# When the lower quarters of w_out's first pair are cast, and where one of their low halves lies

## The chip, the cores and the metric

The kernel runs on one core of one Trainium2 chip. The metric is the device time of one execution in microseconds (us). A profiled execution has a span, from its first to its last instruction, and a time of its own, a little longer than the span.

## The reference

One layer over 2048 new frames and 32 continuing ones, with 1024 features per frame, all float32:

- a normalised frame times w_in gives six streams; a gated short convolution and a pooling mixer turn them into `concat[yA, yB]`, 1024 wide
- `h = h + concat[yA, yB] @ w_out`
- `gate = sigmoid(rmsnorm(h) @ w_ple_gate)`, then `h = h + (p @ w_ple) * gate`
- a last rmsnorm gives the outputs, and the streams' states are returned as well

The change lies in the beginning of the second step, the product with w_out.

## The kernel before

**Precision.** Each float32 operand is split in two float32r parts: `hi` is a copy by ScalarE (ACT), `lo = src - hi` a subtraction by VectorE (DVE). A product is then three matmuls: hi·hi, lo·hi and hi·lo.

**The stages in order.** First the products with w_in (which write y = concat[yA, yB] to the memory tensor `y_d`) with the weights' and frames' splits beside them; then a short piece of the embedding product `p @ w_ple` (three chunks `e`, each stored from a tile `eout` to `e_d`, the first two from ACT's queue, the third from POOL's); then w_out over the frames; then the rest of the embedding product; then the gate.

**w_out, pair by pair.** Two tiles of 128 frames make a pair, and eight pairs follow each other (`for i in range(0, NT - 1, 2)`; pairs o0, o2, o4, ...). Frames and weights are cut in quarters 11, 12, 21, 22, and `seven` computes the pair by Strassen's scheme with seven products instead of eight. Each is 4 x 3 = 12 matmuls of 128x128 by 128x512, so a pair is 84. The frames' parts are y_11, y_12, y_22 and the sums S1 to S4 (`y_fS` the float32 sum on DVE, then `y_S` its hi on ACT and lo on DVE); the weights' are 11, 21, 22 (tiles wo_c and wo_d) and the sums T1 to T4 (wo_a, wo_b, wo_T). The PSUM banks are called x_o, y_o, z_o. In the first pair (`late=True, first_tile=True`) `seven` does, in program order: X = 11·11; carry c1; `step(1)`; first half of Z = S1·T1; X += S2·T2; carry c2 (c_o); second half of Z; carry c3; `step(4)`; Z += S4·22; X += S3·T3; Y = 12·21; X += 22·T4. The scheduler puts S3·T3 and Y ahead of S4·22. In the first pair a carry is a copy on ACT (line 1320) and an addition to x on DVE (line 1315); in the later pairs it is one addition on DVE.

**The quarters of w_out for the first pair.** T1 to T4 and 11 are ready when the pair begins. The bottom rows of w_out are loaded into four tiles wo_q (`bots`, line 317) just before, on SP's queue, and cast by `layout`: per row block one ACT cast (line 1388) and one DVE subtraction (line 1389) for the lower left quarter 21 and the same for the lower right 22. `rest`, called by `step(1)`, does it: it calls `more()`, which prepares y_12, S4 and y_22, and asks for `layout(["21", "22"])` to be issued after y_22's cast.

**Pools and queues.** `w3` holds the three tiles d1, d0, d2 of the quarters (d2 is the low half of 22, d0 that of 21). `qa` holds two tiles `gs`, into which rows of the gate's weights are loaded by POOL's queue (line 1367) to be scaled by ACT (line 1371). Both pools lie where the first stage's tiles, among them the three `eout`, lay. SP's queue (q1 in the profile's DMA windows; POOL's is q0, ACT's q10) carries, in this order: the four wo_q loads, x of the first pair's second tile, y of the second pair in two halves (line 309), x of the second pair twice, y of the third pair in two halves, and so on. After each pair the prep of the next but one frames' parts begins (`prep_h`).

Of the kernel before, what the change touches and what calls it, by code (L numbers as in the profile page):

```python
# [10 lines left out]
F32R = mybir.dt.float32r  # L11
AF = mybir.ActivationFunctionType
ALU = mybir.AluOpType
PSUM = bass.MemoryType.PSUM

P = 128
# [11 lines left out]
NH = D // 2  # L28
KH = KC // 2
# [5 lines left out]
def trunk(ctx, tc, x_p, x_s, c_conv, c_pool, p_p, p_s, g_mix, w_in, conv_w, conv_b, pool_w,  # L35
# [18 lines left out]
    def bank(name):  # L54
        return ps_m.tile([P, 512], F32, tag="mm", name=name)
# [22 lines left out]
    def split(hi, lo, src, eng=nc.vector, later=False):  # L78
        ins = nc.scalar.copy(hi, src)  # L79
        if later:  # L80
            tc.keep_in_program_order(ins)
        eng.tensor_tensor(lo, src, hi.bitcast(F32), op=ALU.subtract)
        return ins
# [65 lines left out]
    def product(ps, lhs, w, n, start, ks=range(KH), order=None):  # L149

        if order is not None:
            steps = [(k, *p) for p in order for k in ks]
            for i, (k, a, b) in enumerate(steps):
                nc.tensor.matmul(ps[:n], lhs[:, k, a, :n], w[b][:, k], start=start and i == 0, stop=i == len(steps) - 1,
                                 skip_group_check=True)
            return
        for k in ks:  # L160
            for q, (a, b) in enumerate(FINE):
                nc.tensor.matmul(ps[:n], lhs[:, k, a, :n], w[b][:, k], start=start and k + q == 0,  # L162
                                 stop=k == KH - 1 and q == 2, skip_group_check=True)
# [11 lines left out]
    def frame_parts(cmb, tmp, name, a11, a12, a21, a22):  # L175

        A = {}  # L180

        def put(q, src):
            A[q] = cmb.tile([P, KH, 2, P], F32R, tag="c", name=f"{name}_{q}")
            return split(A[q][:, :, 0], A[q][:, :, 1], src)

        def comb(q, x, y, op):
            t = tmp.tile([P, KH, P], F32, tag="s", name=f"{name}_f{q}")
            nc.vector.tensor_tensor(t, x, y, op=op)
            return t

        s1 = comb("S1", a21, a22, ALU.add)
        put("11", a11)
        s2 = comb("S2", s1, a11, ALU.subtract)
        put("S2", s2)
        put("S1", s1)
        put("S3", comb("S3", a11, a21, ALU.subtract))

        def more():
            put("12", a12)
            put("S4", comb("S4", a12, s2, ALU.subtract))  # L200
            return put("22", a22)

        return A, more

    def seven(name, A, W, carry, out, between={}, late=False, in_parts=False, first_tile=False):

        step = lambda c: between[c]() if c in between else None
        frames_late, weights_late = (FINE, FINE[::2] + FINE[1:2]) if in_parts else (None, None)
        X, Y, Z = (bank(f"{c}_{name}") for c in "xyz")

        def lower(*parts):
            for ks in parts:
                product(Z, A["S1"], W["T1"], P, ks.start == 0, ks)
            return carry(Z, (1, 1)) if ks.stop == KH else None  # L220

        parts = range(KH // 2), range(KH // 2, KH)
        product(X, A["11"], W["11"], P, True, order=frames_late)
        c1 = carry(X, (0, 0))
        step(1)

        def upper():
            product(Y, A["12"], W["21"], P, True, order=weights_late)
            out(Y, c1, (0, 0))

        if not late:
            upper()
        if late:
            lower(parts[0])
        step(2)
        product(X, A["S2"], W["T2"], P, False)
        c2 = carry(X, (0, 1))
        step(3)
        c3 = lower(parts[1]) if late else lower(range(KH))
        step(4)  # L240

        def right():
            product(Z, A["S4"], W["22"], P, False, order=weights_late)
            out(Z, c2, (0, 1))

        if first_tile:
            right()
        product(X, A["S3"], W["T3"], P, False)
        out(X, c3, (1, 1))
        step(5)  # L250
        if late:
            upper()
        if not first_tile:
            right()
        step(6)
        product(X, A["22"], W["T4"], P, False)
        out(X, None, (1, 0))
# [29 lines left out]
    def slot(name):  # L287
        return acts[0].tile([P, SLOT], F32R, tag="hn", name=name)
# [8 lines left out]
    def sums_slots(name):  # L297
        a, b = halves(slot(f"{name}_a")), halves(slot(f"{name}_b"))
        t4 = seventh(f"{name}_T4").rearrange("p (h k n) -> p h k n", h=2, k=KH)
        return dict(T1=a[:2], T2=(a[2], b[0]), T3=b[1:], T4=(t4[:, 0], t4[:, 1]))  # L300
# [24 lines left out]
    with ExitStack() as s1:  # L325
        pool = lambda name, bufs: s1.enter_context(tc.tile_pool(name=name, bufs=bufs))
# [16 lines left out]
        def put(piece, src, later=False):  # L343

            split(piece[:, :, 0], piece[:, :, 1], src, later=later)
# [905 lines left out]
        for gi, tbs in enumerate(GROUPS):  # L1251
            if gi == 2:
# [6 lines left out]
                W = sums_slots("wo")  # L1259
# [35 lines left out]

    with ExitStack() as s2:
        pool = lambda name, bufs: s2.enter_context(tc.tile_pool(name=name, bufs=bufs, reuse_waits="tile"))
        w3, qa, xh, st, ss, cmb = (pool(*a) for a in (
            ("w3", 1), ("qa", 2), ("xh", 3), ("st", 4), ("ss", 3), ("cmb", 8)))

        def quarters(name, W):
            c = halves(slot(f"{name}_c"))
            d = {h: w3.tile([P, KH, NH], F32R, tag=f"d{h}", name=f"{name}_d{h}") for h in (1, 0, 2)}
            W.update({"11": c[:2], "21": (c[2], d[0]), "22": (d[1], d[2])})

        def whole_quarters(W, k, top, bot):
# [6 lines left out]
        def h_ops(x, n, name, bare=False, two=False):  # L1313

            add = lambda o, a, b: nc.vector.tensor_tensor(o, a, b, op=ALU.add)  # L1315

            def carry(ps, at):
                t = st.tile([P, NH], F32, tag="t", name=f"c_{name}_{at[0]}{at[1]}")
                if bare and at != (1, 0):
                    nc.scalar.copy(t[:n], ps[:n])  # L1320
                    return t
                add(t[:n], ps[:n], half_of(x, at, n))
                if two:
                    add(t[:n], ps[n:2 * n], t[:n])
                return t

            def out(ps, c, at):
                t = half_of(x, at, n)
                if bare and at != (1, 0):
                    add(t, t, c[:n])  # L1330
                    c = None
                add(t, ps[:n], t if c is None else c[:n])
                if two:
                    add(t, ps[n:2 * n], t)

            return carry, out
# [46 lines left out]
        def layout(parts):  # L1383
            for k in range(KH):
                for q, t, c in ("11", tops[k // 2], k % 2), ("21", bots[k], 0), ("22", bots[k], 1):
                    if q in parts:
                        hi, src = W[q][0][:, k], t[:, c * NH:c * NH + NH]
                        nc.scalar.copy(hi, src)
                        hold.append(nc.vector.tensor_tensor(W[q][1][:, k], src, hi.bitcast(F32), op=ALU.subtract))
# [1 line left out]
        quarters("wo", W)  # L1391
        layout(["11"])

        def rest():

            with tc.issue_after(more().ins):
                layout(["21", "22"])

        S = {}
        more = prep_h(0)  # L1400
# [9 lines left out]
        for i in range(0, NT - 1, 2):  # L1410
            with tc.issue_after(loaded[-1].ins):
                x = [load_rows(xh, "x", i + b, x_p) for b in range(2)] if i else [first_x, second_x]
            seven(f"o{i}", S.pop(i), W, *h_ops(x, P, f"o{i}", i == 0), {0: {1: rest}, 2: {3: next_gate}}.get(i, {}), True, i == 0)
            for b in range(2):
                done_h(i + b, x[b])
            last = i + 4 == NT - 1
            if last:
                n = tiles[NT - 1][1]
                A = short("yl", load_y(NT - 1, n), n)
            if i + 2 < NT - 1:  # L1420

                with tc.issue_after(loaded[-1].ins), tc.issue_after(hold[-1].ins):
                    more = prep_h(i + 2)
                more()
            if last:
                x = load_rows(xh, "x", NT - 1, x_p, x_s)
                plain("ol", A, W, n, *h_ops([x], n, "ol", two=True))
                done_h(NT - 1, x)
            next_gate()
# [29 lines left out]
        W = sums_slots("wg")  # L1459
# [204 lines left out]
        S = {}  # L1664
# [7 lines left out]
        h, e = (load_rows(*a) for a in ((xh, "h", NT - 1, h_d), (ya, "e", NT - 1, e_d)))  # L1672
        plain("gl", A, W, n, *short_ops(h, e, n))
        done_g(NT - 1, h)
        for i in range(0, NT - 3, 2):
            A = S.pop(i)
            h = [load_rows(xh, "h", i + b, h_d) for b in range(2)]
# [34 lines left out]
```

## Time and profile before

| what | before |
|---|---|
| median of 3 runs | 923.92 us (922.3 to 926.05) |
| span of the profiled execution | 923.4 us |
| its own time | 925.15 us |
| TensorE busy | 908.2 us, 98% |
| VectorE busy | 723.8 us, 78% |
| ScalarE busy | 483.5 us, 52% |
| DMA | 201.98 MB, 219 GB/s on the mean |

PE is TensorE's matmul, DVE VectorE, ACT ScalarE, POOL GpSimd, SP the engine that issues loads. A row of a timeline is: start, duration, engine, line, operation, output<-inputs (buffer numbers left out), shapes, count, and in brackets how long the engine stood idle before it and what ended that. A chain row is: start, duration, what. All starts are in us from the span's start. The first pair of w_out runs from 546.6 to 567.1 us.

### The profile page before, as it was taken

Reading aid. Unit: us, or ns where it says so; the run is one execution under the profiler, and the core shown is the slowest. Engines: PE = TensorE matmul, PEld = TensorE weight load, DVE = VectorE, ACT = ScalarE, POOL = GpSimd, SP = SyncE. Lnnn points to the kernel's source line nnn. Section 1 sums busy time; section 2 is a strip of 40 time slices with the busy share of each in tenths; the row PEclk is TensorE's granted clock in tenths of the full one; section 3 lists DMA queues with packets and bytes.
Section 4 is the critical chain, followed back from the end, with each engine's and each line's share of the span. In section 5 each row is a group of like instructions: output and inputs, shape, how many; then the busy total and the mean of one; then the engine's idle time right before and its main releaser. Section 6 shows DMA issues by size and latency. Waiting matters only on the chain.

```text
span 923.4 us, 13197 instructions
## 1 busy us (share of the span) xinstructions
PE 908.2 (98%) x4521; PEld 823.2 (89%) x4521; DVE 723.8 (78%) x1237; ACT 483.5 (52%) x895; POOL 160.5 (17%) x303
## 2 busy tenths in 40 slices
PE   8999999999999999999999999999999999999996
PEld 6999998999999999999999987888878868888885
DVE  6996898999576989795777669665558658889885
ACT  6744565654345555443545446334336755565563
POOL 2111222121000332210000010111203201111123
PEclk9999999999999999999999999999999999999999
DMA  8357687898945799638975359866777964676653
GB/s 245 100 143 218 168 247 224 244 281 283 417 138 170 236 237 229 213 124 292 273 240 171 104 206 270 271 184 186 222 241 232 371 233 137 230 255 199 204 195 114
DMA packets 137679, 201.98 MB, mean 219 GB/s; under 512 B 13116, under 2 KB 101724, under 8 KB 136333
## 3 DMA queue, kind: packets, MB, share of 16 engines
q1 hardware_dynamic: 117581, 138.36, 48.4%
q0 software_dynamic: 17296, 57.35, 19.2%
q10 hardware_dynamic: 2736, 5.44, 1.8%
q8 instruction: 35, 0.57, 0.3%
q14 instruction: 31, 0.25, 0.1%
HBM read 135.55 MB, written 65.54 MB: 218 GB/s over the span
## 4 chain that ended last, share of the span: by engine, by line
PE 76%; DVE 6%; DMA 3%; issue 1%; ACT 1%; POOL 1%; POOLq 0%; DVEq 0%; ACTq 0%
PE x_g L162 9%; PE x_o L162 8%; PE x_zab L574 6%; PE e L106 5%; PE x_zbv L574 5%; PE z_g L162 4%; PE x_ch L574 4%; PE z_o L162 4%; PE z_zab L574 3%; PE z_zbv L574 2%; PE z_ch L574 2%; PE y_g L162 2%; PE y_o L162 2%; PE h L574 2%; PE zb L574 2%; PE c L574 2%
## 5 line engine op out<-in xcount | busy, mean ns | idle before, releaser
L79 ACT CAST y_S<-y_fS 128x512 fp32r<-128x512 f32 x32 | 19.5, 622 | 42.2 <-PE x_o L162 20.4
L162 PE MATMUL x_g<-wg_b,g_S 128*128 128x512 f32 x128 | 36.7, 392 | 0.0
L106 PE MATMUL e<-wq,pps 128*128 128x512 f32 (+1 forms) x156 | 36.2, 391 | 0.1
L162 PE MATMUL x_o<-wo_b,y_S 128*128 128x512 f32 x128 | 35.8, 391 | 0.0
L106 PEld LDWEIGHTS e<-wq,pps 128*128 128x128 f32 (+1 forms) x156 | 28.2, 182 | 7.5 <-issue 0.5
L574 PE MATMUL x_zab<-B,w_zab_S 128*128 128x416 f32 x168 | 34.2, 352 | 0.2 <-ACT V L970 0.2
L574 PE MATMUL z_zab<-B,w_zab_S 128*128 128x416 f32 x168 | 34.3, 351 | 0.0
L574 PE MATMUL x_zbv<-B,w_zbv_S 128*128 128x416 f32 x168 | 34.2, 352 | 0.0
L574 PE MATMUL z_ch<-B,w_ch_S 128*128 128x416 f32 x168 | 34.1, 351 | 0.0
L574 PE MATMUL z_zbv<-B,w_zbv_S 128*128 128x416 f32 x168 | 34.0, 351 | 0.0
L574 PE MATMUL x_ch<-B,w_ch_S 128*128 128x416 f32 x168 | 34.0, 351 | 0.0
L574 PEld LDWEIGHTS x_zab<-B,w_zab_S 128*128 128x128 f32 x168 | 31.3, 188 | 0.9 <-ACT V L970 0.5
L574 PEld LDWEIGHTS x_ch<-B,w_ch_S 128*128 128x128 f32 x168 | 31.4, 188 | 0.3
L574 PEld LDWEIGHTS z_zbv<-B,w_zbv_S 128*128 128x128 f32 x168 | 31.4, 188 | 0.3
L574 PEld LDWEIGHTS z_ch<-B,w_ch_S 128*128 128x128 f32 x168 | 31.3, 188 | 0.3
L574 PEld LDWEIGHTS z_zab<-B,w_zab_S 128*128 128x128 f32 x168 | 31.3, 188 | 0.3
L574 PEld LDWEIGHTS x_zbv<-B,w_zbv_S 128*128 128x128 f32 x168 | 31.3, 188 | 0.4
L79 ACT CAST y<-y 128x512 fp32r<-128x512 f32 x24 | 14.8, 618 | 29.6 <-PE z_o L162 12.8
L71 POOL TENSOR_SCALAR ms_f<-ssq_f 128x1 f32<-128x1 f32 (+1 forms) x15 | 7.6, 509 | 129.4 <-ACT junk L92 129.4
L1315 DVE TENSOR_TENSOR c_o<-x_o,x 128x512 f32<-128x512 f32 x14 | 9.7, 690 | 25.0 <-PE x_o L162 25.0
L162 PEld LDWEIGHTS x_o<-wo_b,y_S 128*128 128x128 f32 x128 | 23.9, 188 | 5.6 <-ACT y_S L79 0.4
L162 PEld LDWEIGHTS x_g<-wg_b,g_S 128*128 128x128 f32 x128 | 23.7, 188 | 4.7
(587 smaller groups left out, 2688.8 us busy)
## 6 DMA issues: line engine op xcount, KB each, us to landing
y<-y_d SPq DMA_DIRECT2D x16, 512.0 KB, 6.0
x<-in_x_prompt_dram SPq DMA_DIRECT2D x16, 512.0 KB, 5.9
h_d<-x SPq DMA_DIRECT2D x16, 512.0 KB, 4.6
h<-h_d SPq DMA_DIRECT2D x16, 512.0 KB, 3.5
xt<-in_x_prompt_dram SPq DMA_DIRECT2D x15, 512.0 KB, 7.1
e<-e_d SPq DMA_DIRECT2D x15, 512.0 KB, 4.8
out_dram<-h POOLq DMA_DIRECT2D x14, 512.0 KB, 3.1
p_dT<-T POOLq DMA_DIRECT2D x12, 512.0 KB, 6.4
```

Source lines behind the costliest of these rows:

```text
L71: nc.gpsimd.tensor_scalar(ms[:n], ssq[:n], scalar1=1.0 / D, scalar2=EPS, op0=ALU.mult, op1=ALU.add)
L79: ins = nc.scalar.copy(hi, src)
L106: nc.tensor.matmul(ps[:n], pps[:, a, k, :n], wp[k][b][:, cs], start=k + q == 0, stop=k == 1 and q == 2)
L162: nc.tensor.matmul(ps[:n], lhs[:, k, a, :n], w[b][:, k], start=start and k + q == 0, stop=k == KH - 1 and q == 2, skip_group_check=True)
L574: nc.tensor.matmul(ps[:, :NB], lhs[:, k, x], b[:, k, y], start=start and k + q == 0, stop=stop and k == KH - 1 and q == 2, skip_group_chec ...
L1315: add = lambda o, a, b: nc.vector.tensor_tensor(o, a, b, op=ALU.add)
```

## The change

`more` is cut in three steps: 0 casts y_12, 1 makes and casts S4, 2 casts y_22. In the first pair `step(1)` now calls `lower_left`: y_12's cast, and behind it the casts of the quarter 21. `step(4)`, behind the three carries, calls `lower_right`: S4, behind its cast the casts of the quarter 22, and then y_22. d2 moves from the pool `w3` to a pool of its own, `w2`, which is opened behind `qa`. In all other places the three steps of `more` follow each other as before.

```diff
-        def more():
-            put("12", a12)
-            put("S4", comb("S4", a12, s2, ALU.subtract))
+        def more(i):
+            if i == 0:
+                return put("12", a12)
+            if i == 1:
+                return put("S4", comb("S4", a12, s2, ALU.subtract))
             return put("22", a22)
...
-        w3, qa, xh, st, ss, cmb = (pool(*a) for a in (
-            ("w3", 1), ("qa", 2), ("xh", 3), ("st", 4), ("ss", 3), ("cmb", 8)))
+        w3, qa, w2, xh, st, ss, cmb = (pool(*a) for a in (
+            ("w3", 1), ("qa", 2), ("w2", 1), ("xh", 3), ("st", 4), ("ss", 3), ("cmb", 8)))
...
-            d = {h: w3.tile([P, KH, NH], F32R, tag=f"d{h}", name=f"{name}_d{h}") for h in (1, 0, 2)}
+            d = {h: (w2 if h == 2 else w3).tile([P, KH, NH], F32R, tag=f"d{h}", name=f"{name}_d{h}") for h in (1, 0, 2)}
...
-        def rest():
-
-            with tc.issue_after(more().ins):
-                layout(["21", "22"])
+
+        def lower_left():
+            with tc.issue_after(more(0).ins):
+                layout(["21"])
+
+        def lower_right():
+            with tc.issue_after(more(1).ins):
+                layout(["22"])
+            more(2)
...
-            seven(f"o{i}", S.pop(i), W, *h_ops(x, P, f"o{i}", i == 0), {0: {1: rest}, 2: {3: next_gate}}.get(i, {}), True, i == 0)
+            seven(f"o{i}", S.pop(i), W, *h_ops(x, P, f"o{i}", i == 0), {0: {1: lower_left, 4: lower_right}, 2: {3: next_gate}}.get(i, {}), True, i == 0)
...
-                more()
+                for part in range(3):
+                    more(part)
```

## Prediction

> **What bounds the kernel now.** The page comes first, then the chain of waits over the stretch that the change touches, then the engines' timelines there, then the DMA windows.
>
> ```profile
> span 923.4 us, 13197 instructions
> PE 908.2 (98%) x4521; PEld 823.2 (89%) x4521; DVE 723.8 (78%) x1237; ACT 483.5 (52%) x895; POOL 160.5 (17%) x303
> PEclk9999999999999999999999999999999999999999
> ```
>
> TensorE is the bound: 98% of the span, at full granted clock. An edit that adds no matmul can win only where PE pauses. The chain of waits from 540 to 610 us:
>
> ```profile
> 549.03 15.00 DMA y<-y_d
> ...
> 564.12 0.69 DVE y_fS L188
> ...
> 570.82 0.61 DVE c_o L1315
> 571.48 3.02 PE x_o L162 x12
> ...
> 575.86 3.00 PE x_o L162 x12
> ...
> 584.31 5.44 PE x_o L162 x24
> ...
> 603.35 5.44 PE x_o L162 x24
> ```
>
> In the first pair of w_out (546.6 to 567.1) the chain is not on PE: it is a load of y for the second pair, landing at 564.0, and then DVE's queue up to the second pair's first carried sum, c_o, which lets PE begin at 571.48. From there on the chain stays on PE. PE's own rows show what it lost:
>
> ```profile
> 546.64 2.96 PE L157 MATMUL x_o<-wo_c,y 128*128 128x512 f32 x12
> ...
> 554.91 3.02 PE L162 MATMUL x_o<-wo_b,y_S 128*128 128x512 f32 x12
> 557.76 1.14 PE L157 MATMUL y_o<-wo_c,y 128*128 128x512 f32 x3
> 559.44 1.42 PE L157 MATMUL y_o<-wo_c,y 128*128 128x512 f32 x5 [0.53 <-ACT wo_c L1388]
> ...
> 564.34 2.88 PE L162 MATMUL x_o<-wo_T,y 128*128 128x512 f32 x12
> 567.06 2.88 PE L162 MATMUL x_o<-wo_c,y 128*128 128x512 f32 x12
> 569.78 1.52 PE L162 MATMUL z_o<-wo_a,y_S 128*128 128x512 f32 x6
> 571.48 0.50 PE L162 MATMUL x_o<-wo_a,y_S 128*128 128x512 f32 x1 [0.18 <-DVE c_o L1315]
> ```
>
> Twelve matmuls take 567.06 - 564.34 = 2.72 us, 0.227 each. A pair has 84, so 19.04 us. The first pair took 567.06 - 546.64 = 20.42, a loss of 1.38: about 1.1 in y_o, which waits for the casts of the lower left quarter (wo_c), and some 0.2 at 554.91 behind a carried sum. The second pair ends at 584.31 + 2.72 = 587.03, so it took 19.97, a loss of 0.93: at 571.48 and at 575.86, both behind carried sums. The third pair, 587.03 to 603.35 + 2.72 = 606.07, took 19.04: no loss. So **2.31 us is all there is**, 0.25% of the span. A measurement of this kernel can tell about 0.5% (4.6 us) from no change.
>
> **Part 1: the lower left quarter earlier.**
>
> ```profile
> 550.12 0.62 ACT L79 CAST y<-y 128x512 fp32r<-128x512 f32 x1
> 553.75 0.62 ACT L79 CAST y_S<-y_fS 128x512 fp32r<-128x512 f32 x1 [3.02 <-PE x_o L162]
> 554.28 0.58 ACT L1320 COPY c_o<-x_o 128x512 f32<-128x512 f32 x1
> ...
> 555.65 0.62 ACT L1388 CAST wo_c<-wo_q 128x512 fp32r<-128x512 f32 x1
> ...
> 559.30 0.62 ACT L1388 CAST wo_d<-wo_q 128x512 fp32r<-128x512 f32 x1
> ```
>
> ACT takes 0.52 us a step in a row of casts ((559.30 - 555.65)/7), and sits idle for 3.02 us before 553.75. In the built program of the changed kernel the four casts of the lower left quarter follow directly on the cast at 550.12: 550.65 to 552.84, inside that idle time. DVE's four subtractions follow 0.60 apart, the last behind the last cast, done by 554.2; PE takes up y_o only at 557.6. So y_o waits for nothing: -1.1. The copy c_o no longer stands behind the cast of 553.75 and starts at 553.73 itself, 0.53 earlier, and ends at 554.31, before PE asks for it at 554.87: -0.2 at 554.91. ACT and DVE do the same number of instructions; the lower right's casts, now one by one behind c_o, S4 and the second copy, end at 557.5 and their subtractions at 558.7, while PE reaches them at 560.3. "22" is cast last, 557.4, its subtraction ends at 559.3, needed at 563.0. So the first pair runs without a pause from 554.87 over its last 48 matmuls (10.88 us) and ends at 565.75 instead of 567.06. The cover of all this is PE's 2.72 us blocks; without it each 0.52 of a cast would cost 0.52.
>
> The new wait: the casts need w_out's bottom rows, and c_o is queued behind them on ACT.
>
> ```profile
> 541.04 2.21 SPq L317 DMA_DIRECT2D wo_q<-in_w_out_dram  x4
> ...
> DMA to landing us min/median/max: 5.7/5.7/5.7
> ...
> q1 hardware_dynamic: 640, 2.36, 63.8%
> ```
>
> The middle line is the second of the four loads, issued at 541.4, so landed at 547.1. The last is SP's queue from 541 to 551.8: 2.36 MB, more than the four loads' 2.10. So the fourth landed by about 552.1 and its cast starts at 552.22: just in time, with 0.9 us to spare before c_o.
>
> **Part 2: the moved pool.** One low half of the lower right goes to a new pool w2 behind qa, so qa, into which the gate's rows (gs) are loaded, moves down in memory. In the built program the first gs load no longer waits for the first embedding store but for the third, which POOL itself issues:
>
> ```profile
> 548.08 0.55 POOL L143 DMA_DIRECT2D e_d<-eout  x1 [11.38 <-ACT y_S L79]
> 549.58 1.43 POOL L1367 DMA_DIRECT2D gs<-in_w_ple_gate_dram  x2 [0.94 <-DMA e_d<-eout]
> ...
> 577.72 0.75 POOL L1367 DMA_DIRECT2D gs<-in_w_ple_gate_dram  x1 [6.21 <-DMA g_d<-gs]
> ...
> 571.96 0.72 ACT L1371 ACTIVATE gs<-gs,vec 128x512 f32<-128x512 f32 x1
> ...
> DMA to landing us min/median/max: 6.8/6.8/6.8
> ...
> DMA to landing us min/median/max: 11.3/12.1/13.0
> ```
>
> The last two lines are that store (landed 554.9) and the two gs loads of 549.58. POOL so issues gs at about 555.5 instead of 549.6; ACT scales it only at 572, and even 13 us bring it in at 569. The direct price is nothing. The indirect one is a gain, since gs slows SP's loads while it runs. Windows 554.5:562.5 (both queues), 562.5:569, 577.7:580.5 and 541:554.5 (SP's queue alone quoted):
>
> ```profile
> q1 hardware_dynamic: 925, 1.27, 78.5%
> q0 software_dynamic: 462, 0.49, 35.0%
> ...
> q1 hardware_dynamic: 1351, 2.09, 93.0%
> ...
> q1 hardware_dynamic: 807, 0.85, 86.2%
> ...
> q1 hardware_dynamic: 955, 2.86, 60.8%
> ```
>
> Beside gs, SP's queue q1 moves 1.27 MB in 8 us, 159 GB/s; without it 2.09 in 6.5, 321 GB/s. The third stretch begins as another gs is issued (577.72) and shows no q0 for 2.8 us, so gs needs that long from issue to its first bytes. By 554.5, 2.86 MB had gone: four bottom loads and one x (2.62) and 0.24 of y; so 2.91 MB (y, y, x, x, y, y of 0.524 each, less 0.24) stand up to the end of the third pair's y. After the change q1 runs nearly alone until 558.3: 1.25 MB at 321 to 370 GB/s, so the second pair's y (0.81 left) lands near 557.5, not 564.0. Then 8 us at 159 GB/s, then 321: the third pair's y lands at about 567.5 to 568; before it was near 569.5 (by 571.34 at the latest, where DVE's first sum on it ran unhindered).
>
> [...]
>
> **Part 3: DVE's order.** This decides.
>
> ```profile
> 564.12 0.69 DVE L188 TENSOR_TENSOR y_fS<-y,y 128x512 f32<-128x512 f32 x1 [1.01 <-DMA y<-y_d]
> ...
> 570.74 0.68 DVE L1315 TENSOR_TENSOR c_o<-x_o,x 128x512 f32<-128x512 f32 x1
> 571.34 0.68 DVE L188 TENSOR_TENSOR y_fS<-y,y 128x512 f32<-128x512 f32 x1
> ```
>
> Before, c_o was the eleventh instruction behind the y_fS of 564.12 (11 x 0.602 = 6.6). In the changed program it is the sixteenth, and two sums on the third pair's y (steps 12 and 13) stand before it. DVE is done with the first pair's share of this (the subtraction of "22" and the sum x<-x_o) at 559.9 and goes on with the second pair's y if that has landed. Counting from there, step 10 needs the first pair's last matmul (565.9), step 12 the third pair's y at 568.0, and c_o ends at 568.05 + 4 x 0.602 + 0.69 = 571.15. PE, which in the new order does 12 + 9 matmuls of the second pair before it needs c_o, is there at 565.75 + 4.76 = 570.5 and waits 0.7. Its next twelve end at 571.2 + 0.13 + 2.72 = 574.05 (0.13 is what its first matmuls behind a wait take longer: 3.02 against 2.88 for twelve in the rows above), four more and the second carried sum let it go on at 575.0, and 0.13 + 2.72 + 35 x 0.227 later the third pair starts at 585.78: 587.03 - 585.78 = **1.25 us earlier**. What PE gains it keeps: from 587 on it is the chain.
>
> The profiled execution took 925.15, so 923.9 after; against the median of 923.92 shown, which lies 1.2 lower, 922.7.
>
> **The rivals.** (1) *The carried sum waits in DVE's queue; slower.* If y does not land earlier, because gs was not what held it, c_o stands sixteenth behind 564.12: it ends at 564.12 + 9.63 + 0.69 = 574.44, PE waits from 570.5 to 574.5, and the third pair starts at 589.07: +2.0 us, 925.9. It decides once the second pair's y lands after 562.0. For it: the load was under way for 15 us, longer than gs was. Against: 159 against 321 GB/s. [...] (2) *Only the order of the loads changes*: the third pair's y at 569.5, c_o at 572.65, third pair at 587.28: +0.25. (3) *No stall at all*: third pair's y by 567.1: -2.1, with 0.2 left for the second carried sum. (4) *The casts wait for the bottom rows*: each us past 553.1 costs one; against it the 2.36 MB. That the order is not what the diff says can be left out: the built program has it.
>
> **How the numbers follow.** Forecast (third pair's y at 567.1 to 569.2, -2.1 to 0): 0.48. (3) 0.12. (2) 0.17. (1) 0.17, of which 0.04 with the clock's fall. (4) and what I do not see: 0.06. All named cases lie within 4.6 us; over it would be only an unseen stall, or the runs' own spread (922.3 to 926.05): same 0.90, slower 0.06, faster 0.04. Range: 923.92 - 2.1 and + 2.0, each widened by about 0.8 for that spread: 921.0 to 926.7.
>
> **What would show it.** Right: no pause at y_o, first pair 19.1 us long and the second about 20.0; gs issued near 555.5; DVE's first sum on the second pair's y before 561; c_o ending near 571. Wrong: that sum still at 564 and c_o at 574 (rival 1); c_o released by the third pair's y near 569.5 (2); ACT idle before a wo_c cast (4); or any PE pause behind 587.

## The result and the profile after

| kernel | median of the runs | ratio to the kernel before, 95% interval |
|---|---|---|
| before | 923.36 us (921.8 to 928.07, 22 runs) | |
| changed | 926.13 us (923.32 to 930.48, 22 runs) | 1.0027 [1.0018, 1.0037] |
| changed, second measurement | 924.88 us (11 runs) | 1.0003 [0.9993, 1.0013] |
| changed, third measurement, on another chip than the second | 926.15 us (12 runs) | 1.0024 [1.0009, 1.004] |

By these ratios the changed kernel is slower by 0.3 to 2.5 us, not faster; the second measurement alone could not be told from no change. Its profiled execution took 926.86 us, with a span of 925.1. PE's timeline of it, around the second pair:

```profile
545.32 2.96 PE L157 MATMUL x_o<-wo_c,y 128*128 128x512 f32 x12
...
556.28 1.98 PE L157 MATMUL y_o<-wo_c,y 128*128 128x512 f32 x8
558.09 1.07 PE L157 MATMUL y_o<-wo_d,y 128*128 128x512 f32 x4
...
564.44 2.88 PE L162 MATMUL x_o<-wo_c,y 128*128 128x512 f32 x12
567.16 2.20 PE L162 MATMUL z_o<-wo_a,y_S 128*128 128x512 f32 x9
572.07 0.63 PE L162 MATMUL x_o<-wo_a,y_S 128*128 128x512 f32 x1 [2.71 <-DVE c_o L1317]
572.50 0.63 PE L162 MATMUL x_o<-wo_b,y_S 128*128 128x512 f32 x1
...
588.24 1.98 PE L162 MATMUL x_o<-wo_c,y 128*128 128x512 f32 x8
```

The first pair now takes 564.44 - 545.32 = 19.12 us, with no pause (20.42 before). The second takes 588.24 - 564.44 = 23.80 (19.81 before, 586.87 - 567.06 by PE's records). From the first pair's first x_o to the third pair's, called the stretch from here on, 42.92 us stand against 40.23: +2.69. What lies behind it is the same within 0.4 us (336.85 against 336.51). This execution reached the first pair 1.32 us earlier than the one of before, so a time of the prediction is met here 1.32 lower.

DVE's timeline says why PE stood still. In the last column is the idle time ahead of an instruction and what ended it:

```profile
558.45 0.68 DVE L188 TENSOR_TENSOR y_fS<-y,y 128x512 f32<-128x512 f32 x1
...
565.29 0.68 DVE L188 TENSOR_TENSOR y_fS<-y,y_fS 128x512 f32<-128x512 f32 x1
568.79 0.69 DVE L188 TENSOR_TENSOR y_fS<-y,y 128x512 f32<-128x512 f32 x1 [2.82 <-DMA y<-y_d]
569.51 0.69 DVE L188 TENSOR_TENSOR y_fS<-y_fS,y 128x512 f32<-128x512 f32 x1
...
571.33 0.68 DVE L1317 TENSOR_TENSOR c_o<-x_o,x 128x512 f32<-128x512 f32 x1
```

The second pair's y came early, as hoped (558.45 instead of 564.12). DVE then ran dry for 2.82 us ahead of the first sum on the third pair's y, and c_o stands four instructions behind that sum. The sum of 568.79 is the first on the third pair's y. The chain of waits goes the same way:

```profile
557.96 10.75 DMA y<-y_d
...
568.79 0.70 DVE y_fS L188
...
571.41 0.61 DVE c_o L1317
...
572.07 4.60 PE x_o L162 x12
```

Twelve matmuls that take 2.72 us elsewhere took 4.60 here. The stretch's windows show the cause; columns: stretch, its length, busy time of PE, PEld, DVE, ACT and POOL, the granted clock of PE, DMA share, GB/s:

```profile
565.46:568.87 3.41, 3.41 (x17) 2.83 (x16) 0.59 (x2) 3.33 (x7) 0.73 (x3) 1.00 1.00 357
568.87:572.28 3.41, 0.70 (x4) 0.28 (x3) 3.38 (x6) 1.23 (x2) 0.00 (x0) 1.00 0.68 260
572.28:575.70 3.42, 3.42 (x9) 2.65 (x9) 1.54 (x3) 0.00 (x0) 1.44 (x2) 0.50 0.94 284
575.70:579.11 3.41, 3.41 (x15) 2.60 (x15) 2.40 (x4) 1.25 (x2) 0.00 (x0) 1.00 1.09 340
```

In the third row the clock is 0.50, which will be called the clock's fall: eight matmuls start 0.427 apart instead of 0.227, which is 8 x 0.20 = 1.6 us. So the second pair lost 2.87 to the pause (from 569.2, where its nine z_o matmuls end, to 572.07), 1.6 to the clock and 0.3 to small steps (19.04 + 4.76 = 23.80).

### The profile page after: what moved, and what is told of

Read it like the earlier page. It is cut to its first block, busy times and chain, and to the rows that moved or that the text cites. A ratio compares the mean times of both kernels' runs of the same rounds, so it can differ in the third digit from the quotient of the medians.

```text
span 925.1 us, 13199 instructions
## 1 busy us (share of the span) xinstructions
PE 908.6 (98%) x4521; PEld 824.8 (89%) x4521; DVE 724.3 (78%) x1237; ACT 483.7 (52%) x895; POOL 161.6 (17%) x303
## 4 chain that ended last, share of the span: by engine, by line
PE 87%; DVE 4%; DMA 3%; ACT 2%; issue 2%; POOL 1%; POOLq 0%; DVEq 0%; SPq 0%; ACTq 0%
PE x_g L162 9%; PE x_o L162 7%; PE x_zbv L576 7%; PE x_zab L576 7%; PE x_ch L576 6%; PE z_g L162 4%; PE z_o L162 3%; PE z_zbv L576 3%; PE z_zab L576 3%; PE e L106 3%; PE h L576 3%; PE z_ch L576 3%; PE b L576 3%; PE za L576 3%; PE zb L576 2%; PE c L576 2%
```

## The experiments

Theory A: c_o is late because, in DVE's queue, it stands behind two sums on the third pair's y, and that y lands late as long as the gate's rows (gs) are being loaded. Theory B: the clock's fall behind the pause is a cost of its own. The rivals to A are that the moved casts themselves hold c_o up (by ACT or by the bottom rows), and to B that the fall costs nothing since a load sets the end anyway, or that it comes from something else.

**The sums asked for behind the carried sum.** The third pair's frame parts are asked for behind the second pair's first c_o, so that c_o leads on DVE:

```diff
-                add(t[:n], ps[:n], half_of(x, at, n))
+                carried.append(add(t[:n], ps[:n], half_of(x, at, n)))
...
-                with tc.issue_after(loaded[-1].ins), tc.issue_after(hold[-1].ins):
+                behind = carried[0].ins if i == 2 else hold[-1].ins
+                with tc.issue_after(loaded[-1].ins), tc.issue_after(behind):
```

> The changed kernel with one edit: the third pair's float32 sums are placed on DVE behind the second pair's first carried sum c_o instead of ahead of it. Measured from the first pair's first x_o to the third pair's first x_o the kernel before took 40.39 us and the changed one 42.91. Theory A (c_o waits because two sums on the third pair's y, which lands late, stand ahead of it in DVE's queue; the pause of 2.87 us this makes on PE also lets its clock fall to half for 3.41 us, 1.6 us more): no pause, clock at 1.0 throughout, stretch 38.2 to 38.6 us, time about 2 us below the kernel before, ratio 0.998. Theory B (DVE is simply behind, c_o would wait for its own turn anyway): pause still 1.5 us or more, stretch above 40 us, ratio 1.000 or above.

> The changed kernel with the third pair's sums asked for behind the second pair's first carried sum, once more, for a narrower interval: the stretch was 38.50 us against 40.23 before, which is 1.7 us or 0.9981 of the time, and the first measurement was 0.9989 with an interval from 0.9979 to 1.0. If what PE gains in the stretch is kept, the two measurements together give 0.998 to 0.999; if something behind gives it back, 1.0.

Measured: 923.02 us, 0.9989 [0.9979, 1.0] over 12 runs, then 922.62, 1.0 [0.9991, 1.0009] over 11. The stretch was 38.50 in both profiles. PE and DVE of the second:

```profile
567.63 1.97 PE L162 MATMUL z_o<-wo_a,y_S 128*128 128x512 f32 x8
569.65 0.50 PE L162 MATMUL x_o<-wo_a,y_S 128*128 128x512 f32 x1
```

```profile
568.92 0.68 DVE L1317 TENSOR_TENSOR c_o<-x_o,x 128x512 f32<-128x512 f32 x1
569.52 0.68 DVE L188 TENSOR_TENSOR y_fS<-y,y 128x512 f32<-128x512 f32 x1
```

With one order changed on DVE the pause shrinks to 0.21 us and 4.4 us of the stretch are back (1.6 of them the clock's fall, which is gone too). This is as A has it: neither the casts nor the bottom rows hold c_o. Against the kernel before, the stretch is 1.7 us shorter, but the time only 0 to 1 us, where about 2 were expected: the gain is not all seen in the whole run.

**The gate's rows later.** The first gs load is held back behind the first pair's rs_h on POOL, and the later ones move with it:

```diff
-        nc.gpsimd.tensor_tensor(r[:n], ms[:n], nhalf[:n], op=ALU.pow)
+        roots.append(nc.gpsimd.tensor_tensor(r[:n], ms[:n], nhalf[:n], op=ALU.pow))
...
-..., 2: {3: next_gate}}.get(i, {}), True, i == 0)
+..., 6: {3: next_gate}}.get(i, {}), True, i == 0)
...
-            next_gate()
+            with tc.issue_after(roots[-1].ins):
+                next_gate()
```

> The changed kernel with the first load of the gate's rows (gs) held on POOL until the second frame tile of the first pair has its root, some 12 us later, and the gate's other loads moved one pair later with it. DVE's order up to c_o stays as in the changed kernel. Theory A (c_o waits for the third pair's y, and that lands late because gs takes the DMA engines while it is loaded): the third pair's y lands 3 us or more earlier, no pause at c_o, clock 1.0, stretch 38.2 to 38.8 us, ratio about 0.998. Theory C (that y is late because its slot comes free late and it is asked for late, whatever gs does): it lands within 1 us of before, the pause of 2 to 3 us stays, stretch 41.5 to 43 us, ratio 1.002 to 1.003.

Measured: 927.08 us, 1.0040 [1.0027, 1.0054]; stretch 38.49, with no fall of the clock in it. DVE's order is that of the changed kernel, and only the landing is another:

```profile
565.98 0.68 DVE L190 TENSOR_TENSOR y_fS<-y,y_fS 128x512 f32<-128x512 f32 x1
566.58 0.68 DVE L190 TENSOR_TENSOR y_fS<-y,y 128x512 f32<-128x512 f32 x1
...
569.14 0.68 DVE L1319 TENSOR_TENSOR c_o<-x_o,x 128x512 f32<-128x512 f32 x1
```

The sum on the third pair's y no longer waits, and c_o starts 2.6 us behind it as in the changed kernel (571.33 - 568.79 = 2.5). The second half of that y was asked for 12.6 us behind the first pair's start in both kernels (558.6 - 546.02 here, 557.96 - 545.32 there), and the sum on it starts 20.6 us behind that start here and 23.5 there, so it is not the asking that made it late, but gs beside it. The whole run, for which a ratio of 0.998 was expected, is slower for another reason, which the edit brought in: the gate's later loads now end late, and the chain at the pair o6 (23.02 us long) begins with one of them.

```profile
610.33 8.86 DMA gs<-in_w_ple_gate_dram
...
619.21 0.73 ACT gs L1375
```

**The casts alone.** The changed kernel without the pool w2; the order on every engine is that of the changed kernel:

```diff
-            d = {h: (w2 if h == 2 else w3).tile([P, KH, NH], F32R, tag=f"d{h}", name=f"{name}_d{h}") for h in (1, 0, 2)}
+            d = {h: w3.tile([P, KH, NH], F32R, tag=f"d{h}", name=f"{name}_d{h}") for h in (1, 0, 2)}
...
```

> The changed kernel with the pool w2 taken back: d2 lies in w3 again, gs is asked for at its old time; the order on every engine is that of the changed kernel. By the prediction's rival 1 the second pair's y lands 17 to 17.5 us after the first x_o, c_o ends near 27.8, PE waits 4 us: stretch 42.4 us at full clock, 44.1 with the clock's fall, ratio 1.002 to 1.004. If instead the moved load of gs is what costs (it only delays the third pair's y), the stretch is at or below that of the kernel before, 39 to 40.4 us, ratio 0.999 to 1.000.

> The kernel with the moved casts alone, again, on the same chip as the next one. Theory: a pause of 3.8 us brings the clock's fall in every run on any chip: granted clock 0.996 or less in every run, stretch near 44.0 us, ratio 1.004 to 1.005. Rival (the fall is a matter of the chip): 0.997 or more in most runs, and a ratio near 1.0025.

Measured: 927.75 us, 1.0051 [1.0038, 1.0064], all 6 runs with a granted clock of 0.995 or 0.996; then on another chip 927.33, 1.003 [1.0018, 1.0042], with 4 of 12 runs so. Stretches 43.99 and 44.76; the first ratio lies above the 1.002 to 1.004 that were expected. Here gs is issued at 548.48, as before the change. POOL, DVE and PE of the first profile:

```profile
548.48 1.44 POOL L1369 DMA_DIRECT2D gs<-in_w_ple_gate_dram  x2 [1.00 <-PE x_o L157]
```

```profile
562.66 0.69 DVE L188 TENSOR_TENSOR y_fS<-y,y 128x512 f32<-128x512 f32 x1 [3.98 <-DMA y<-y_d]
...
572.67 0.68 DVE L1317 TENSOR_TENSOR c_o<-x_o,x 128x512 f32<-128x512 f32 x1
```

```profile
567.85 1.88 PE L162 MATMUL z_o<-wo_a,y_S 128*128 128x512 f32 x7
573.41 0.50 PE L162 MATMUL x_o<-wo_a,y_S 128*128 128x512 f32 x1 [3.68 <-DVE c_o L1317]
```

This is the prediction's first rival at work: the second pair's y lands late, past 562.0, and c_o stands sixteenth behind it. PE paused for 3.84 us in the first profile, where about 4 were expected. That the clock falls in every run with such a pause was my expectation, and it failed: on the second chip two runs in three went without.

**The pool alone.** The kernel before with w2:

```diff
-            d = {h: w3.tile([P, KH, NH], F32R, tag=f"d{h}", name=f"{name}_d{h}") for h in (1, 0, 2)}
+            d = {h: (w2 if h == 2 else w3).tile([P, KH, NH], F32R, tag=f"d{h}", name=f"{name}_d{h}") for h in (1, 0, 2)}
...
```

> The kernel before with the pool w2 alone: gs waits for the third embedding store, the order on every engine is that of the kernel before. Theory A: y_o still waits 1.1 us for its casts, first pair 20.4 us; the second pair's y lands early, so DVE reaches c_o about 1 us sooner and the pause before it goes; the third pair's y, late, stands behind c_o and holds nothing: stretch 39.5 to 40.0 us, ratio 0.999 to 1.000. If the moved load alone made the loss: stretch 41.5 us or more, ratio 1.002 or above.

> The kernel before with the pool of its own for d2 alone, once more: its stretch was 39.49 us against 40.23, 0.7 us or 0.9992 of the time, and the first measurement was 1.0003 with an interval from 0.9994 to 1.0011. If the gain of the stretch is kept: 0.999 to 1.0. If it is given back behind the third pair: 1.0 or more, and the rest of its span behind the third pair's start is then longer than the before kernel's 336.5 us by that much.

Measured: 924.04 us, 1.0003 [0.9994, 1.0011], then 923.16, 0.9999 [0.9991, 1.0008]; stretches 39.49 and 39.47 (pairs 20.43 + 19.06 in the first). With the old order on DVE the later gs load takes away the second pair's loss and leaves the first pair's. The stretch's 0.75 us do not show in the time, and what lies behind the stretch is not longer for it (336.18 and 336.58 against 336.51), so they are not given back there. Put together:

| stretch, us | casts as before | casts moved |
|---|---|---|
| d2 as before | 40.23, again 40.12 | 43.99, 44.76 |
| d2 in w2 | 39.49, 39.47 | 42.92, 42.20, 44.00 |

The casts' move costs 2.7 to 4.6 us of the stretch by what it does to DVE's order, the clock's fall included, and the pool gives back about 1.

**Matmuls in the pause.** Unused matmuls of the same size, on PE in the second pair behind the first six of z_o; 12 in the changed kernel, 18 in the kernel with the casts alone:

```diff
+        if name == "o2":
+            idle = tbank("idle")
+            for _ in range(12):
+                tc.keep_in_program_order(nc.tensor.matmul(idle, A["11"][:, 0, 0], W["11"][0][:, 0], start=True, stop=True,
+                                                          skip_group_check=True))
```

> The changed kernel, with 12 more matmuls of the same size (their results are not used) put on PE in the second pair behind the first six of z_o, so in the pause in which PE waits for the second pair's first carried sum. They take 12 x 0.227 = 2.72 us and displace three matmuls that did run in the pause (0.68 us). Theory (the clock falls because PE stands still for 2.9 us): no granted clock of 0.5 behind the pause, mean granted clock 0.997 or more in every run, and the stretch from the first pair's first x_o to the third pair's is 42.92 - 1.6 + 0.7 = 42.0 us; the whole run about 1 us shorter than the changed kernel's slower group (926.9), ratio to the kernel before 1.0015 to 1.003. Rival (the clock's fall comes from something else, such as the load on the whole core): the fall is still there and the stretch is 43.6.

> The changed kernel with the 12 unused matmuls in the pause, once more. Its stretch was 41.32 us with no fall of the clock, 1.1 above before, and yet the first measurement gave 1.0040 over 6 runs from 924.7 to 929.0 us. If that was the chance of few runs: 1.001 to 1.003 now, granted clocks all 0.997 or more. If the matmuls themselves make something dearer that varies from run to run (the pause itself, say, longer than in the profile): 1.004 again, with a stretch over 42 in the second profile.

> The kernel with the moved casts alone (no pool of its own for d2), with 18 unused matmuls put on PE at the same place, in a pause of 3.8 us. Theory (standing still is what makes the clock fall, and the fall cost that kernel 1.6 us in every run): granted clock 0.997 or more in every run where without them all were 0.995 or 0.996, stretch 43.99 - 1.6 + 0.7 = 43.1 us. Rival (clock falls anyway): stretch 44.7, clocks of 0.995 and 0.996 as before. Rival (the fall costs nothing on the whole, since the chain is then on a load): time unchanged at a ratio of 1.005.

> The kernel with the moved casts and 18 unused matmuls in the pause, on the same chip as the one ahead. If the clock's fall costs the whole run what it costs the stretch (42.24 against 43.99): 1.0 to 1.8 us shorter than the kernel ahead, with all granted clocks at 0.997 or more. If the matmuls cost as much elsewhere as the fall does: the same time as the kernel ahead, within 0.5 us.

Measured, 12 matmuls: 926.66 us, 1.004 [1.0027, 1.0054], and 926.72, 1.0027 [1.0017, 1.0036]; stretches 41.32 and 41.80 (the first ratio above what was expected, the second within). With 18: 927.09, 1.0044 [1.0031, 1.0057], and 926.91, 1.0031 [1.002, 1.0043]; stretches 42.24 and 43.00. The granted clock was 0.997 or more in all 34 runs. PE with 18 of them, in the last of these profiles:

```profile
566.61 1.71 PE L162 MATMUL z_o<-wo_a,y_S 128*128 128x512 f32 x6
568.15 4.25 PE L241 MATMUL idle<-wo_c,y 128*128 128x512 f32 x18
572.69 0.50 PE L162 MATMUL x_o<-wo_a,y_S 128*128 128x512 f32 x1 [0.28 <-DVE c_o L1322]
```

So here it was standing still that made the clock fall: 18 of the changed kernel's 45 runs and 10 of the 18 with the casts alone had a clock of 0.996 or less, and none of the 34 filled ones. What the fall costs a whole run was to be told by the pair on one chip, casts alone and filled. 1.0 to 1.8 us were expected between them, and 0.42 were measured (927.33 and 926.91), which is what the rival had, that the matmuls cost as much as the fall does. The casts alone took 929.2 us in its 4 runs with a clock of 0.996 or less (median) and 926.8 in the other 8. By this split a run with the fall is 2.4 us longer, and the filling saves that where the clock would have fallen and nothing where not. But the runs were split after the fact, by a clock that is the mean of a whole run, and a longer pause may go with the fall: in its profile the fall lasted 6.83 us, not 3.41. So that the fall costs the stretch 1.6 us is shown, and that it costs the whole run about 2 is likely, not shown. In the changed kernel the filling does not pay either: on one chip it took 926.72 against 924.88, where 10 of the 11 unfilled runs had kept their clock. The displaced matmuls (0.7 us) explain part of that 1.8; the rest stays open.

**Both kernels again.**

> The kernel before itself, once more, for a second profile. In the profiles so far the stretch from the first pair's first x_o to the third pair's is 40.23 us before, but timed kernels come out 0.8 to 2.4 us above what their stretches give against it. Theory S (the loads of y land at other times in other executions, and the one profile of before was a dear one): the stretch is 39.0 to 39.7 here. Rival F (the stretch is always 40.2, and the front before the first pair, which begins anywhere from 544.2 to 547.6, holds the difference): 40.2 again, with another start of the first pair. Ratio 1.0 by both.

> The changed kernel itself, once more. Theory (pause of 2 to 4 us on c_o behind the third pair's y, clock's fall in some executions alone): stretch 40.9 to 43.5, with a granted clock of 0.5 near 572 where it is over 42.5 and without where it is under 41.5; c_o released by DVE, and DVE's sum ahead of it by a load of y. Ratio 1.002 to 1.0035.

> The changed kernel a third time, since two measurements on different chips gave 1.0027 (10 of 22 runs with a granted clock of 0.996 or less) and 1.0003 (1 of 11). Theory: its cost is 0.5 to 1.1 us for the late sum and 1.7 us more where the clock falls, so the ratio goes with the share of runs at 0.996: 1.0005 to 1.0015 where they are few, 1.002 to 1.003 where they are half or more. Rival: the ratio does not go with that share.

Measured: before 923.63 us, 1.0002 [0.9991, 1.0012], stretch 40.12, so the one profile of before was not a dear one. Its first pair began at 547.73, and over all kernels here it began between 544.22 and 547.73: even two profiles of one kernel differ there by 1.8 us (547.62 and 545.79 with the sums behind the carried sum). So one profile's span says nothing of a 2 us change, while the stretch does. The changed kernel: stretches 42.20 and 44.00, pauses of 2.15 and 3.93 us, the clock's fall behind both. In all its 45 runs 18 had a clock of 0.996 or less, median 927.01; the other 27, 924.95. The 115 runs of the kernel before in these experiments have a median of 923.76, three of them at 0.996 or less. By this split the late sum costs 1.2 us and a run with the fall some 2 more. The three measurements of the changed kernel go with its share of such runs: 11 of 22 (1.0027), 1 of 11 (1.0003), 6 of 12 (1.0024), as expected, though each of the two parts would need more runs to be sized well.

## Why the prediction was wrong

**What bounds the kernel** held, with a slip of 0.16 us: 587.03 took the chain's piece for the third pair's start, where PE's record has 586.87. The second pair's loss was 0.77 and the whole 2.15, not 2.31.

**Part 1** held. The four casts of the lower left run on ACT at 549.32 in one row (2.18 us), y_o waits for nothing, and the first pair takes 19.12 where 19.1 was forecast.

**Part 2** failed in its last term. gs was issued at 553.74 (forecast 555.5, here 554.2) and the second pair's y was there by 558.45, both as forecast:

```profile
553.74 1.43 POOL L1369 DMA_DIRECT2D gs<-in_w_ple_gate_dram  x2 [6.41 <-PE z_o L162]
```

The third pair's y was put at 567.5 to 568, so 566.2 to 566.7 here; its second half landed at 568.7, and in the other two profiles of the changed kernel the sum on it starts 0.7 us earlier and 1.1 later, measured from the first pair's start. The rate was nearly right. SP's queue in the windows 539.7:553.2, 553.2:557.1, 557.1:564.8 (with gs beside it) and 564.8:568.7 of the changed kernel:

```profile
q1 hardware_dynamic: 1043, 2.95, 61.9%
...
q1 hardware_dynamic: 942, 1.51, 106.7%
...
q1 hardware_dynamic: 974, 1.15, 76.4%
q0 software_dynamic: 518, 0.51, 38.3%
...
q1 hardware_dynamic: 840, 1.30, 101.4%
```

Beside gs 1.15 MB in 7.7 us are 149 GB/s (159 forecast). Up to the end of the third pair's y eleven loads of 0.524 MB had to go, 5.77 MB; 5.61 had gone by 564.8, and at 1.30 MB in 3.9 us the rest takes 0.5. By the count of bytes, then, y was due at 565.3, and it landed 3.4 us later, when 6.91 MB had gone: the queue's next transfers went by. **The step that failed is the count itself: it took a queue's bytes for bytes that land in order.** Beside gs they did not. The profile of before had shown it: by the same count the second pair's y, 0.81 MB at 159 GB/s behind 554.5, was due at 559.6, and it landed at 564.03, 4.4 us later. In the one profile without gs beside it the count came nearer: with the gate's rows later 5.74 MB had gone by 561.9, and the first half of the third pair's y, the tenth load (5.24 MB by the count), landed at 551.75 + 10.3 = 562.05. A sum that doesn't give back the landing in the trace should not have been trusted for the next one. What held the last part up isn't in the records.

The second rival, by which only the order of the loads changes, was nearer: the second pair's y did come earlier (the sum on it 13.1 us behind the first pair's start, 17.5 before), and the third pair's stood at 568.7 + 1.3 = 570.0, where the rival has 569.5. In part that was luck. The 569.5 was put down for the kernel before, and the prediction's own count does not give it: 1.64 MB (2.91 less 1.27) at 321 GB/s behind 562.5 are there at 567.6. The first half did land at 552.69 + 15.4 = 568.1; of the second the profile tells only that it was there by 571.34. Counted alike, before and after, the later gs promised this load nothing (567.6 and 567.5 to 568). And the rival's price of +0.25 had no fall of the clock in it.

**Part 3** held in its order and failed with its input. c_o was the sixteenth step, four behind the sum; it ended at 572.02 where the forecast, moved by 1.32, has 569.83. PE was there at 569.2, as forecast, and waited 2.87 instead of 0.7.

**The clock.** The forecast gives its fall a chance of 0.04, and no run ahead of the forecast shows how long a fall behind a pause lasts or what it costs. The runs showed 0.50 for 3.41 us, 1.6 us in the stretch, and that all three profiled executions of the changed kernel fell, behind pauses of 2.87, 2.15 and 3.93 us. The page's row of nines can hide a fall: 3.41 us at 0.50 take 0.07 from a slice of 23.1 us, and the changed kernel's row has a nine there too. Nor had PE stood still through the whole of the 3.41 us ahead: it was busy for 0.70 us in the window ahead of the fall above, and for 1.42 in the second profile of the changed kernel:

```profile
569.46:572.87 3.41, 1.42 (x6) 0.86 (x5) 3.41 (x6) 1.16 (x2) 0.00 (x0) 1.00 0.85 317
572.87:576.28 3.41, 3.41 (x9) 2.64 (x8) 0.75 (x2) 0.00 (x0) 1.44 (x2) 0.50 1.00 325
```

In numbers: forecast -1.25, measured +2.69 in the profiled executions, 3.94 apart; 2.2 of it is the late y, 1.6 the clock, and 0.16 the slip named first. The chance of 0.90 for less than 0.5% either way held (1.0027), the sign did not, and 926.13 lies within the range, near its upper end, for which a rival's price had set the bound.

## What to carry to other kernels

When a step is moved, the place in an in-order queue that the others get is the change: look at what then stands ahead of the step that PE waits for, and let nothing that hangs on a load stand there (one order on DVE was worth 4.4 us of the stretch, with the clock's fall that it brought). Before a load's landing is forecast from bytes and rates, give back with the same sum a landing that the trace shows, and compare a counted time with one counted alike. PE's pauses of 2.15 to 3.93 us cost the pause here and, in a part of the runs, 1.6 us more for the clock in the stretch (about 2 by the medians of the runs).

## What was not expected of the hardware

In the profiles here the clock's falls sat on a grid. The times at full clock ahead of them lasted 559.79 us in the first profile of the changed kernel, 563.20 in its two others and in both of the casts alone, and 143.36 ahead of a fall in the front of the first carry-first profile; in the profile of before it was 907.95, up to 919.00, with the last matmul done by 916.1. Divided by 164, 165, 42 and 266 they all give 3.413 us, which is what the fall itself lasted (once 6.83, where PE was still idle as it began). If a fall begins at no other time, a pause's place on that grid counts beside its length, which would explain that only a part of the runs falls; this is an estimate from these numbers, and it was not tried by shifting a pause. The casts-alone kernel shows both sides in one pause of 3.84 us, and its second profile the long fall:

```profile
567.89:571.31 3.42, 1.84 (x8) 1.20 (x7) 3.38 (x6) 2.13 (x5) 1.33 (x3) 1.00 0.93 361
571.31:574.72 3.41, 1.31 (x6) 1.09 (x7) 3.41 (x7) 3.01 (x6) 1.17 (x2) 1.00 0.99 270
574.72:578.13 3.41, 3.41 (x10) 2.63 (x9) 0.79 (x2) 0.29 (x1) 0.54 (x1) 0.50 0.91 278
```

```profile
568.98:572.39 3.41, 0.64 (x3) 0.19 (x1) 3.38 (x7) 2.94 (x6) 1.86 (x3) 1.00 0.82 279
572.39:575.81 3.42, 2.72 (x6) 2.16 (x7) 2.50 (x5) 1.60 (x3) 0.00 (x0) 0.50 0.95 285
575.81:579.22 3.41, 3.41 (x9) 2.65 (x8) 0.60 (x1) 0.60 (x1) 0.75 (x1) 0.50 1.03 357
```

With 1.84 us busy in a window the clock stayed, with 1.31 in the next it fell. The busy time alone does not settle it: in the second profile of before, in the front, a window with 2.35 us busy was followed by a fall at 16.54, and the window ahead of it, with 1.90, was not.

Not settled: the stretches of the carry-first and pool-only kernels are 1.7 and 0.75 us shorter than before's in each of two profiles, and their times follow by half of that or less. No kernel tried beats the kernel before by more than its interval in both of its measurements.
